# Score pairs read behind their products, one bank for transposed weights, and TensorE's rows as written, in the attention of an encoder layer

## The chip, the cores and the metric

The kernel runs on one core of a Trainium2 chip. The metric is the time of one execution on the device in microseconds (us), as the median of several runs; lower is better. A core has five engines that work side by side, each through its own queue of instructions in a fixed order: TensorE (PE in the profile, with its weight loads as PEld) multiplies matrices and transposes, VectorE (DVE), ScalarE (ACT) and GpSimd (POOL) work on elements, and SyncE (SP) issues transfers (DMAs). An instruction that needs another engine's result waits on a semaphore, and everything behind it in its queue waits with it. Products are written to PSUM, which the kernel cuts into eight banks of 128 x 512 numbers.

## The reference

One layer of an encoder for 1024 positions of 1024 features, in float32. A projection feeds two branches, a gated MLP (A) and eight heads of attention (B). Each head attends with three patterns of window and dilation, whose results are joined by their softmax denominators.

```python
PATTERNS = ((128, 1), (512, 4), (2048, 16))

def mixture_of_dilations(q, k, v):
    slopes = alibi_slopes(N_HEADS_B)
    outs, lses = [], []
    for _, dilation in PATTERNS:
        o, l = dilated_window_attention(q, k, v, dilation, slopes)
        outs.append(o)
        lses.append(l)
    w = jax.nn.softmax(jnp.stack(lses, axis=0), axis=0)
    o = jnp.stack(outs, axis=0)
    return jnp.sum(w[..., None].astype(o.dtype) * o, axis=0)

def hybrid_layer(x, w_in, b_gate, g_pre, g_post, ln_g, ln_b, w_s, b_s, w_pa, w_pb, w_o):
    h = rms_norm(x, g_pre)
    proj = h @ w_in
    u_a, v_a, z_a, q_b, k_b, v_b, z_b, gate_a, gate_b = jnp.split(proj, SPLIT_OFFS, axis=-1)
    y_a = spatial_gating(jax.nn.gelu(u_a), jax.nn.gelu(v_a), ln_g, ln_b, w_s, b_s) * jax.nn.silu(z_a)
    ...
    m = g_a * (y_a @ w_pa) + g_b * (y_b @ w_pb)
    return x + rms_norm(m @ w_o, g_post)
```

## The kernel before

Each float32 product is made of three products of halves: high times high, high times low, low times high. `split` (L158) makes the halves, the high one (names that end in h) on ACT at L159, the low one (l) on DVE or POOL at L160. The kernel first makes the projections, then runs the attention, and ends with the products by `w_pb` and `w_o` and the last norm. Beside the attention, whose rows on TensorE are short, it works off the product `y_a @ w_pa` of the MLP branch.

The eight banks of PSUM are handed out by name (L66): two to the MLP's sums (`mm`), three to scores (`sc`), one to transposes (`tp`) and two to the sums of weighted values (`pv`). A bank is free again when its last reader is done.

For each head h:

- `queries_keys` loads and splits q (`qr`, `qc`), and loads the halves of the keys (`krh`, `krl`, L595) and three tables of biases (`ta`, `te`, `tb`, L599).
- `scores` makes eight pairs of score tiles: six products (L662 to L664) for each pair, or twelve narrower ones for the last pair (first and last chunk). At L665 DVE adds the bias and takes the row's extreme; at L669 ACT takes the exponential and its sum, into the weights `st`. In the names, sc610 is the pair of head 6, first kind, tiles 0 and 1; the last pair reads the table `te`.
- `exchange` (L682) brings the extremes and sums of one pattern into the other's order with 16 small copies on POOL and 16 on DVE, `normalise` (L692 to L700) makes the joint factors `nm` on DVE, with an exponential `dd` on ACT, and `scale` (L706 to L710) multiplies the weights by them; eight tiles of it fall to DVE.
- `weigh` makes the weighted sum of values in nine stages. In each, `keys` (L724 to L732) transposes up to four tiles of weights with TensorE into one bank (L728), and splits it into `pth` (ACT) and `ptl` (DVE). Two stages later (`LAG`) the products with v follow, for the first four stages at L747 (sums `pr`), for the others at L762 (sums `pc`). The stages are called b0 to b3 (residues), a1 and a3 (chunks), e (ends), a5 and a7; with the head's number, pb30 is the first of head 3, pa25 the eighth of head 2.

`keys` takes its bank by turns from `tp` and from `sc`:

```python
                pt = bank(turn[0], f"p{name}")
                turn.reverse()
```

The loop at L900 to L926 writes the stages of head h with the score pairs of head h + 1 (`PAIRS`), the loads for head h + 2, and steps of the MLP (`BESIDE`) among them. A step is three products of 128 x 512 (L870 to L872) of a tile of w_pa with a quarter `ya` of the MLP's values; ya0310 is a quarter for the first half of the positions. The eighth, b = 1 in the names (ya1...), come later. Ahead of the loop, head 0's scores run among MLP steps alone.

The rows are not issued as written. A scheduler of the framework runs over the whole program with its own estimate of times, and sets the order of every engine's queue, TensorE's and SP's among them.

Of the kernel before, what the change touches and what calls it, by code (L numbers as in the profile page):

```python
# [13 lines left out]
ALU = mybir.AluOpType  # L14
# [9 lines left out]
H = 8  # L24
# [12 lines left out]
def tile_hybrid_encoder(  # L37
# [39 lines left out]
    def bank(tag, name):  # L77
        return psum.tile([P, 512], F32, tag=tag, bufs=BUFS[tag], name=name)
# [61 lines left out]
    def take(steps, n=None):  # L140

        while n is None or n > 0:
            if next(steps, steps) is steps:
                break
            if n is not None:
                n -= 1
# [433 lines left out]
    with tc.tile_pool(name="heads", bufs=1) as hp, tc.tile_pool(name="attn", bufs=1) as ap:  # L580
        def queries_keys(h, res):

            def pair(nm, shape):
                return [hp.tile([P] + shape, F32R, tag=f"{nm}{s}", name=f"{nm}{s}{h}") for s in "hl"]

            res["qr"], res["qc"], res["kr"] = pair("qr", [4, 256]), pair("qc", [8, P]), pair("kr", [4, 256])
            for b in range(2):
                t = wpool.tile([P, 512], F32, tag="ws", bufs=2, name=f"q{h}{b}")
                nc.sync.dma_start(t, q_d[h][:, 512 * b:512 * (b + 1)])
                split(*[w[:, :, b * P:(b + 1) * P] for w in res["qr"]], t.rearrange("p (j r) -> p r j", r=4))  # L590
                split(*[w[:, 4 * b:4 * b + 4, :].rearrange("p a (r i) -> p a r i", r=4) for w in res["qc"]],
                      t.rearrange("p (a i r) -> p a r i", a=4, r=4), nc.gpsimd)
                yield
            for s in range(2):
                nc.sync.dma_start(f32(res["kr"][s]), k_d[h][:, s])  # L595
                yield
            for x, terms, shape in (("ta", alibi_a, [P, 256]), ("te", alibi_e, [P, 2, 192]), ("tb", alibi_b, [P, 384])):
                res[x] = hp.tile(shape, F32, tag=x, name=f"{x}{h}")
                nc.sync.dma_start(res[x], terms[h])  # L599

        def residue_values(h, res):

            res["vb"] = []
            for s, vd in enumerate((v_hi, v_lo)):
                b_ = ap.tile([P, 4, 2, E], F32R, tag=f"vb{s}", name=f"vbt{s}{h}")
                vt_ = vd.rearrange("(b j r) n -> j r b n", b=2, r=4)
                for bb in range(2):
                    nc.sync.dma_start(f32(b_[:, :, bb, :]), vt_[:, :, bb, h * P:(h + 1) * P])
                res["vb"].append(b_)
# [16 lines left out]
        def scores(h, res):  # L626

            qr, qc, kr, ta, te, tb = [res[n] for n in ("qr", "qc", "kr", "ta", "te", "tb")]  # L630
            own = res["own"] = hp.tile([P, 2, 8, 2], F32, tag="own", bufs=2, name=f"own{h}")
            wts = res["wts"] = {}
            order = [(1, (i, i + 1)) for i in (0, 2, 4, 6)] + [(0, (1, 2)), (0, (3, 4)), (0, (5, 6)), (0, (0, 7))]
            for half, pair in order:
                ps = bank("sc", f"sc{h}{half}{pair[0]}").rearrange("p (t n) -> p t n", t=2)
                st = (hp if half else ap).tile([P, 2, 256], F32, tag=f"st{half}", bufs=7, name=f"st{h}{half}{pair[0]}")
                n = 256
                for t, idx in enumerate(pair):
                    if half:
                        b, r = divmod(idx, 4)  # L640
                        lhs = [w[:, r, b * P:(b + 1) * P] for w in qr]
                        blocks = [(0, 256, [w[:, r, :] for w in kr])]
                        bias = tb[:, P * (1 - b):P * (1 - b) + 256]
                    else:
                        lhs = [w[:, idx, :] for w in qc]
                        if idx in (0, 7):
                            w0, n, j0 = (64, 192, 0) if idx == 0 else (P, 192, 208)
                            blocks = [(0, w0, [w[:, :, j0:j0 + w0 // 4] for w in kr]),
                                      (w0, n - w0, [w[:, :, j0 + w0 // 4:j0 + n // 4] for w in kr])]
                            bias = te[:, t, :]  # L650
                        else:
                            j0 = 32 * idx - 16
                            blocks = [(0, 256, [w[:, :, j0:j0 + 64].rearrange("p r (u i) -> p u r i", u=2)
                                                for w in kr])]
                            bias = ta
                    for c0, w, rhs in blocks:
                        dst = ps[:, t, c0:c0 + w]
                        if len(rhs[0].shape) == 3:
                            dst = dst.rearrange("p (r i) -> p r i", r=4)
                        elif len(rhs[0].shape) == 4:  # L660
                            dst = dst.rearrange("p (u r i) -> p u r i", u=2, r=4)
                        nc.tensor.matmul(dst, lhs[0], rhs[0], start=True, stop=False)  # L662
                        nc.tensor.matmul(dst, lhs[0], rhs[1], start=False, stop=False)
                        nc.tensor.matmul(dst, lhs[1], rhs[0], start=False, stop=True)  # L664
                    nc.vector.tensor_tensor_reduce(st[:, t, :n], ps[:, t, :n], bias, -1.0, -NEG, ALU.add, ALU.min,  # L665
                                                   own[:, half, idx, 0:1])
                for t, idx in enumerate(pair):
                    wts[half, idx] = st[:, t, :n]
                    nc.scalar.activation(st[:, t, :n], st[:, t, :n], AF.Exp, bias=own[:, half, idx, 0:1], scale=-1.0,  # L669
                                         accum_out=own[:, half, idx, 1:2])  # L670
                yield
# [44 lines left out]
        def weigh(h, res):  # L716
# [5 lines left out]

            def keys(jobs, n, w, name):

                pt = bank(turn[0], f"p{name}")
                turn.reverse()
                for c0, src in jobs:
                    nc.tensor.transpose(pt[:n, c0:c0 + P], src, ident)  # L728
                hi = ap.tile([P, 512], F32R, tag="pth", bufs=LAG + 1, name=f"pth{name}")
                lo = ap.tile([P, 512], F32R, tag="ptl", bufs=LAG + 1, name=f"ptl{name}")  # L730
                split(hi[:n, :w], lo[:n, :w], pt[:n, :w])
                return hi, lo  # L732


            pr, turn = {}, ["tp", "sc"]

            def residue(r):
                pw = keys([(256 * kb + P * b, wts[1, 4 * b + r][:, kb * P:(kb + 1) * P])
# [143 lines left out]
        ya = {}  # L882
        take(mlp_tiles(0, 0, ya))
        steps = mlp_products(ya)
        heads = [{} for _ in range(H + 1)]
        take(queries_keys(0, heads[0]))
        take(steps, 8)
        residue_values(0, heads[0])
        chunk_values(0, heads[0])
        for _ in scores(0, heads[0]):  # L890
            take(steps, 1)
        take(exchange(0, heads[0], 0))
        take(exchange(0, heads[0], 1))
        normalise(0, heads[0])
        for tile_ in TILES[0] + TILES[1]:
            scale(heads[0], *tile_)
        for _ in queries_keys(1, heads[1]):
            take(steps, 3)
        before = iter(())
        for h in range(H):  # L900
            more = h + 1 < H
            pairs = scores(h + 1, heads[h + 1]) if more else iter(())
            ahead = queries_keys(h + 2, heads[h + 2]) if h + 2 < H else iter(())
            stages = weigh(h, heads[h])
            for i in range(9):
                take(stages, 1)
                take(before, 1)
                for j in range(BESIDE[i]):
                    if j < PAIRS[i]:
                        take(pairs, 1)  # L910
                    take(steps, 1)
                if i == 3 and more:
                    residue_values(h + 1, heads[h + 1])
                    take(exchange(h + 1, heads[h + 1], 0))
                    late = exchange(h + 1, heads[h + 1], 1)
                if more and i in (6, 7):
                    take(late, 1)
                if more and i == 8:
                    normalise(h + 1, heads[h + 1])
                    for tile_ in TILES[0] + TILES[1]:  # L920
                        scale(heads[h + 1], *tile_)
                    chunk_values(h + 1, heads[h + 1])
                if i > 4:
                    take(ahead, 1)
            take(ahead)
            before = stages  # L926
        for _ in before:
            take(steps, 3)


    with tc.tile_pool(name="tail", bufs=1) as tp:
# [147 lines left out]
```

## Time and profile before

| what | us |
| --- | --- |
| median of three runs | 1573.42 |
| lowest and highest run | 1571.92, 1582.71 |
| the profiled execution | 1580.57 |
| span of the profiled execution | 1578.8 |
| first transposes of weights of head 0 | start at 1058.65 |
| last transposes of weights of head 7 | start at 1364.3 |
| granted clock of TensorE, mean | 0.982 |

A row of the profile's timeline gives the start, the time until the end, the engine, the line, the operation, what it writes and reads, the shape, and in brackets how long the engine was idle ahead of it and what ended that. Names are without the numbers of heads there: all of pb00 to pb73 read "pb". A row of the waits names the waiting engine and line, what it waited for, and the total, the count and the longest. A window's row gives the busy time of each engine in that stretch, TensorE's granted clock, and the share of the DMA engines. Durations of products overlap: TensorE starts one product while the one before drains, so the step from start to start tells what a row costs.

### The profile page before, as it was taken

The numbers are of one execution on the slowest core, as the hardware profiler recorded it, in microseconds if no ns is written. First come the engines' busy times: TensorE is split into PE (matmuls) and PEld (weight loads), VectorE is DVE, ScalarE is ACT, GpSimd is POOL, SyncE is SP. The second block draws the span as 40 slices with busy tenths as digits, with TensorE's granted clock in tenths as the row PEclk, the third lists the DMA queues.
The fourth block names the chain that finished last, engine by engine and source line by source line (L and its number), as shares of the span: only waits on it lengthen the run. The fifth ranks groups of instructions, "written<-read, shape, count | busy, mean of one in ns | idle before, by whom it ended". The sixth has DMA issues, their size and how long they took to land.

```text
span 1578.8 us, 22737 instructions
## 1 busy us (share of the span) xinstructions
PE 1519.4 (96%) x7863; PEld 1280.5 (81%) x7863; DVE 862.8 (55%) x1698; ACT 688.2 (44%) x1315; POOL 778.6 (49%) x711
## 2 busy tenths in 40 slices
PE   8999999999999999999999999989998889999998
PEld 4787999988888888788788888867887778878886
DVE  5722544476665664856665555476667657232112
ACT  5522433343433434343444444576666656341111
POOL 2412644465655555555655555456444455473132
PEclk9999999999999999999999999999999989999999
DMA  8454333344534442535444343587676776885531
GB/s 260 156 172 173 128 107 102 111 127 130 170 117 150 133 162 94 168 121 160 139 132 129 125 148 113 163 245 234 196 205 173 201 226 180 227 278 166 194 107 67
DMA packets 247940, 252.16 MB, mean 160 GB/s; under 512 B 14312, under 2 KB 187400, under 8 KB 247568
## 3 DMA queue, kind: packets, MB, share of 16 engines
q1 hardware_dynamic: 247456, 249.88, 50.7%
q8 instruction: 62, 1.02, 0.3%
q10 hardware_dynamic: 368, 0.82, 0.2%
q14 instruction: 54, 0.44, 0.1%
HBM read 174.10 MB, written 76.55 MB: 159 GB/s over the span
## 4 chain that ended last, share of the span: by engine, by line
PE 72%; DVE 8%; issue 5%; ACT 4%; DMA 4%; POOL 3%; SPq 1%; DVEq 0%; ACTq 0%; POOLq 0%
PE pa L870 2%; PE pa L871 2%; PE pb L994 2%; PE pb L995 2%; PE pb L993 2%; PE pa L872 2%; PE sg L527 2%; PE vb L154 1%; PE vb L156 1%; PE vb L155 1%; ACT st L669 1%; POOL out L1014 1%; PE pr L747 1%; DMA vn<-v_d 1%; DVE vn L516 1%
## 5 line engine op out<-in xcount | busy, mean ns | idle before, releaser
L108 POOL TENSOR_TENSOR wl_pa<-wr_pa,wh_pa 128x512 fp32r<-128x512 f32 x56 | 72.6, 1308 | 61.7 <-ACT wh_pa L106 53.3
L669 ACT ACTIVATE st<-st,own 128x256 f32<-128x256 f32 (+1 forms) x128 | 63.0, 493 | 38.4 <-DVE own L665 37.9
L516 DVE TENSOR_SCALAR vn<-vn,mean,rstd 128x128 f32<-128x128 f32 x128 | 54.9, 483 | 36.9 <-DMA vn<-v_d 36.5
L993 PE MATMUL pb<-yh,wh_pb 128*128 128x512 f32 x128 | 50.0, 390 | 1.7 <-ACT yh L159 1.7
L994 PE MATMUL pb<-yl,wh_pb 128*128 128x512 f32 x128 | 50.1, 391 | 0.4 <-DVE yl L160 0.2
L106 ACT ACTIVATE wh_pa<-wr_pa 128x512 fp32r<-128x512 f32 x64 | 38.6, 625 | 26.6 <-PE pa L871 12.6
L995 PE MATMUL pb<-yh,wl_pb 128*128 128x512 f32 x128 | 49.8, 389 | 0.0
L1028 ACT ACTIVATE sq<-o 128x512 f32<-128x512 f32 x16 | 9.6, 598 | 74.7 <-PE o L1026 74.7
L160 POOL TENSOR_TENSOR vl<-vn,vh 128x512 fp32r<-128x512 f32 x32 | 41.3, 1291 | 0.8 <-ACT vh L159 0.8
L665 DVE CUSTOM_DVE_ANT_0 st<-sc,tb 128x256 f32<-128x256 f32 x64 | 25.5, 421 | 28.9 <-PE sc L664 23.6
L997 POOL TENSOR_TENSOR mb<-thb,mb 128x512 f32<-128x512 f32 x16 | 20.6, 1287 | 41.8 <-DVE thb L996 32.2
L682 DVE COPY oth<-own 32x4 f32<-32x4 f32 x128 | 34.3, 268 | 12.3 <-ACT st L669 10.6
L160 POOL TENSOR_TENSOR qcl<-q,qch 128x512 fp32r<-128x512 f32 x16 | 27.9, 1756 | 26.3 <-ACT qch L159 26.3
L728 PE MATMUL pb<-ident,st 128*128 128x128 f32 x128 | 23.3, 294 | 16.2 <-DVE ptla L160 11.5
L815 POOL TENSOR_TENSOR o<-o,zt 128x512 f32<-128x512 f32 x16 | 20.6, 1295 | 36.2 <-DMA zt<-z_d 18.0
L1008 DVE TENSOR_TENSOR sso<-sso 128x1 f32<-128x1 f32 x8 | 1.3, 160 | 67.6 <-ACT sq L1028 67.6
L682 POOL COPY oth<-own 32x4 f32<-32x4 f32 x128 | 23.9, 187 | 24.3 <-ACT st L669 19.4
L728 PEld LDWEIGHTS pb<-ident,st 128*128 128x128 f32 x128 | 16.7, 150 | 21.9 <-DVE ptla L160 13.2
L165 POOL TENSOR_TENSOR sso<-sso,mhalf 128x1 f32<-128x1 f32 x8 | 4.4, 550 | 59.1 <-DVE sso L164 59.1
L108 POOL TENSOR_TENSOR wl_wos<-wr_wos,wh_wos 128x512 fp32r<-128x512 f32 x16 | 20.7, 1292 | 22.8 <-ACT wh_wos L106 22.8
L160 DVE TENSOR_TENSOR ptlb<-pb,pthb 128x512 fp32r<-128x512 f32 x32 | 21.9, 688 | 16.3 <-ACT pthb L159 16.1
L108 POOL TENSOR_TENSOR wl_vb<-wr_vb,wh_vb 128x512 fp32r<-128x512 f32 x14 | 18.2, 1310 | 25.0 <-ACT wh_vb L106 25.0
(2643 smaller groups left out, 5870.6 us busy)
## 6 DMA issues: line engine op xcount, KB each, us to landing
wr_pa<-in_w_proj_a_dram SPq DMA_DIRECT2D x32, 512.0 KB, 5.1
wr_g<-in_w_in_dram SPq DMA_DIRECT2D x16, 512.0 KB, 3.7
wr_va<-in_w_in_dram SPq DMA_DIRECT2D x16, 512.0 KB, 3.7
wr_u<-in_w_in_dram SPq DMA_DIRECT2D x16, 512.0 KB, 4.1
wr_z<-in_w_in_dram SPq DMA_DIRECT2D x16, 512.0 KB, 3.8
vn<-v_d SPq DMA_DIRECT2D x32, 256.0 KB, 2.7
y_d<-s SPq DMA_DIRECT2D x32, 256.0 KB, 3.1
wr_yf<-y_d SPq DMA_DIRECT2D x16, 512.0 KB, 6.3
```

The costliest lines, as they stand in the source:

```text
L106: nc.scalar.activation(hi, src, AF.Copy)
L108: low.tensor_tensor(lo, src, f32(hi), ALU.subtract)
L160: low.tensor_tensor(lo, src, f32(hi), ALU.subtract)
L516: nc.vector.tensor_scalar(vn[:, c, :], vn[:, c, :], mean[:, 4 * b + c, 0:1], rstd[:, 4 * b + c:4 * b + c + 1], op0=ALU.subtract, op1=ALU.mult)
L527: nc.tensor.matmul(pg[:, 256 * c:256 * (c + 1)], w[:, 2 * cp + c, :], wst, start=(w is vh and c == 0), stop=(w is vl and c == 1), skip_gro ...
L669: nc.scalar.activation(st[:, t, :n], st[:, t, :n], AF.Exp, bias=own[:, half, idx, 0:1], scale=-1.0, accum_out=own[:, half, idx, 1:2])
L682: (nc.gpsimd, nc.vector)[half].tensor_copy(dst, src)
L728: nc.tensor.transpose(pt[:n, c0:c0 + P], src, ident)
L870: nc.tensor.matmul(pss[m], lh[:, k, :], rh, start=(q == 0 and k == 0), stop=False)
L993: nc.tensor.matmul(ps, lh, rh, start=(k == 0), stop=False)
L994: nc.tensor.matmul(ps, lh, rl, start=False, stop=False)
L995: nc.tensor.matmul(ps, ll, rh, start=False, stop=(k == KT - 1))
```

## The change

Three things change, all in the attention.

1. `scores` multiplies both tiles of a pair before DVE reads either. Before, the read of the first tile stood between the two tiles' products.
2. `keys` always takes the bank `tp`. The three banks `sc` then serve scores alone, and each stage's transposes have to wait until the subtraction `ptl` of the stage before has read the bank.
3. From the loads of head 0 to the last stage of head 7, TensorE's queue has the order in which the program is written. The scheduler still orders the other engines' queues. The loop is moved into the block without a change.

```diff
@@ scores
-                n = 256
+                n, biases = 256, []
                 for t, idx in enumerate(pair):
...
                         nc.tensor.matmul(dst, lhs[1], rhs[0], start=False, stop=True)
-                    nc.vector.tensor_tensor_reduce(st[:, t, :n], ps[:, t, :n], bias, -1.0, -NEG, ALU.add, ALU.min,
+                    biases.append(bias)
+                for t, idx in enumerate(pair):
+                    nc.vector.tensor_tensor_reduce(st[:, t, :n], ps[:, t, :n], biases[t], -1.0, -NEG, ALU.add, ALU.min,
                                                    own[:, half, idx, 0:1])
@@ keys
-                pt = bank(turn[0], f"p{name}")
-                turn.reverse()
+                pt = bank("tp", f"p{name}")
...
-            pr, turn = {}, ["tp", "sc"]
+            pr = {}
@@ the loop over the heads
-        heads = [{} for _ in range(H + 1)]
-        take(queries_keys(0, heads[0]))
...
+        with tc.manual_schedule(engines={mybir.EngineType.PE}):
+            heads = [{} for _ in range(H + 1)]
+            take(queries_keys(0, heads[0]))
...
```

Lines behind the two added ones in `scores` move by one or two numbers: L728 becomes L729, L870 to L872 become L871 to L873.

What this does to the queues shows at three places. The first is TensorE's queue ahead of head 0's first transposes (pb00), before; the names in it are the MLP's sums (pa00, pa01), the quarters ya0201 and ya0310, and the weights wh and wl.

```order
L872 MATMUL pa01_9839<-ya0201h_9758,wl_pa0110_9749 128x512
L728 MATMUL pb00_10109<-ident_69,st010_9828 128x128 [waits DVE_49]
L747 MATMUL pr00_10201<-pthb00_10114,vbt10_9803 128x256 [waits DMAHW3_49]
L728 MATMUL pb02_10192<-ident_69,st012_9844 128x128 [waits DVE_49]
L747 MATMUL pr00_10201<-ptlb00_10115,vbt00_9800 128x256 x2
L870 MATMUL pa00_9751<-ya0310h_9858,wh_pa0011_9741 128x512 [waits Activation_49]
L871 MATMUL pa00_9751<-ya0310l_9859,wh_pa0011_9741 128x512 [waits DVE_49]
L872 MATMUL pa00_9751<-ya0310h_9858,wl_pa0011_9743 128x512
```

The same place in the change:

```order
L871 MATMUL pa00_9753<-ya0310h_9860,wh_pa0011_9743 128x512 [waits Activation_49]
L872 MATMUL pa00_9753<-ya0310l_9861,wh_pa0011_9743 128x512 [waits Pool_49]
L873 MATMUL pa00_9753<-ya0310h_9860,wl_pa0011_9745 128x512
L871 MATMUL pa01_9841<-ya0201h_9760,wh_pa0110_9749 128x512
L873 MATMUL pa01_9841<-ya0201h_9760,wl_pa0110_9751 128x512
L729 MATMUL pb00_10111<-ident_69,st010_9830 128x128
L662 MATMUL sc110_10123<-krh1_10032,qrh1_10028 128x256 [waits DMAHW2_49,PE_49]
L663 MATMUL sc110_10123<-krl1_10033,qrh1_10028 128x256 [waits DMAHW4_49]
```

The 12 products with ya0310 moved from behind pb00 and pb02 to ahead of the 12 of pa01 with ya0201, so 36 MLP products stand between head 0's last scores and pb00 where 24 stood; the scores of head 1 follow pb00 directly.

The second place is TensorE's queue at the end of head 2, from the stage a5 to the first stage of head 3, before:

```order
L728 MATMUL pa25_11394<-ident_69,st203_10732 128x128
L762 MATMUL pc20_11359<-ptla23_11299,va02_11006 128x256
L872 MATMUL pa06_11426<-ya0000h_9661,wl_pa0600_10950 128x512
L728 MATMUL pa27_11439<-ident_69,st205_10751 128x128 [waits DVE_49]
L762 MATMUL pc21_11360<-ptle2_11356,ve02_11007 128x128
L728 MATMUL pb30_11508<-ident_69,st310_11057 128x128 [waits DVE_49]
```

and in the change:

```order
L729 MATMUL pa25_11396<-ident_69,st203_10734 128x128 [waits DVE_49]
L763 MATMUL pc20_11361<-ptla23_11301,va02_11008 128x256
L873 MATMUL pa06_11428<-ya0000h_9661,wl_pa0600_10952 128x512
L729 MATMUL pa27_11441<-ident_69,st205_10753 128x128 [waits DVE_49]
L763 MATMUL pc21_11362<-ptle2_11358,ve02_11009 128x128
L729 MATMUL pb30_11510<-ident_69,st310_11059 128x128 [waits DVE_49]
```

The rows stand as before, but the waits are for other work. pa25 now waits for ptle2, pa27 for ptla25 (before for ptle2), and pb30 for ptla27 (before for ptla25).

The third place is SP's queue of transfers for heads 5 and 6, before:

```order
L595 DMA krh6_12336<-k_d_90 128x1024 [waits DMAHW0_49,PE_49]
L622 DMA ve05_12480<-vb_h_84 16x2x128 [waits PE_49]
L621 DMA va05_12479<-vb_h_84 32x7x128 [waits DMAHW3_49,PE_49]
L621 DMA va15_12489<-vb_l_85 32x7x128 [waits DMAHW7_49]
L622 DMA ve15_12490<-vb_l_85 16x2x128 [waits DMAHW0_49]
L595 DMA krl6_12337<-k_d_90 128x1024 [waits DMAHW1_49]
```

and in the change:

```order
L595 DMA krh6_12338<-k_d_90 128x1024 [waits DMAHW0_49,PE_49]
L622 DMA ve05_12482<-vb_h_84 16x2x128 [waits PE_49]
L622 DMA ve15_12492<-vb_l_85 16x2x128 [waits DMAHW0_49]
L595 DMA krl6_12339<-k_d_90 128x1024 [waits DMAHW1_49]
L599 DMA te6_12504<-in_alibi_e_dram 128x384 [waits DMAHW3_49]
L621 DMA va05_12481<-vb_h_84 32x7x128 [waits DMAHW3_49,PE_49]
```

The eight loads va moved from ahead of krl6 to behind it; the eight loads ve stay ahead of it, and the first of them waits for the products pc of head 4 that end before pb50. On TensorE the pair sc610, which needs krh6 and krl6, stood behind pb50, the products pc41 and 13 MLP products, with its rows that need krl6 further back; it moved to directly behind pb50 and six of the products pc41.

More of the change, by code (lines that the diff above doesn't have):

```diff
@@ L884, in tile_hybrid_encoder @@
         steps = mlp_products(ya)
-        heads = [{} for _ in range(H + 1)]
-        take(queries_keys(0, heads[0]))
[L887 to L926, printed above, removed]
@@ L927, in tile_hybrid_encoder @@
-        for _ in before:
-            take(steps, 3)
+        with tc.manual_schedule(engines={mybir.EngineType.PE}):
+            heads = [{} for _ in range(H + 1)]
+            take(queries_keys(0, heads[0]))
+            take(steps, 8)
+            residue_values(0, heads[0])
+            chunk_values(0, heads[0])
+            for _ in scores(0, heads[0]):
+                take(steps, 1)
+            take(exchange(0, heads[0], 0))
+            take(exchange(0, heads[0], 1))
+            normalise(0, heads[0])
+            for tile_ in TILES[0] + TILES[1]:
+                scale(heads[0], *tile_)
+            for _ in queries_keys(1, heads[1]):
+                take(steps, 3)
+            before = iter(())
+            for h in range(H):
+                more = h + 1 < H
+                pairs = scores(h + 1, heads[h + 1]) if more else iter(())
+                ahead = queries_keys(h + 2, heads[h + 2]) if h + 2 < H else iter(())
+                stages = weigh(h, heads[h])
+                for i in range(9):
+                    take(stages, 1)
+                    take(before, 1)
+                    for j in range(BESIDE[i]):
+                        if j < PAIRS[i]:
+                            take(pairs, 1)
+                        take(steps, 1)
+                    if i == 3 and more:
+                        residue_values(h + 1, heads[h + 1])
+                        take(exchange(h + 1, heads[h + 1], 0))
+                        late = exchange(h + 1, heads[h + 1], 1)
+                    if more and i in (6, 7):
+                        take(late, 1)
+                    if more and i == 8:
+                        normalise(h + 1, heads[h + 1])
+                        for tile_ in TILES[0] + TILES[1]:
+                            scale(heads[h + 1], *tile_)
+                        chunk_values(h + 1, heads[h + 1])
+                    if i > 4:
+                        take(ahead, 1)
+                take(ahead)
+                before = stages
+            for _ in before:
+                take(steps, 3)
```

## Prediction

> **What bounds the kernel now.** I read the page first: busy time by engine, then the chain that ended last.
>
> ```profile
> span 1578.8 us, 22737 instructions
> PE 1519.4 (96%) x7863; PEld 1280.5 (81%) x7863; DVE 862.8 (55%) x1698; ACT 688.2 (44%) x1315; POOL 778.6 (49%) x711
> PE 72%; DVE 8%; issue 5%; ACT 4%; DMA 4%; POOL 3%; SPq 1%; DVEq 0%; ACTq 0%; POOLq 0%
> ```
>
> TensorE (PE) is busy for 96% of the span and no other engine for more than 55%: the kernel is bound by TensorE's rows, and only gaps between them can be won or lost. The change touches the attention alone, 1028 to 1365 us, so the next view is busy time and granted clock there, by 40 us.
>
> ```profile
> 1100.00:1140.00 40.00, 38.62 (x238) 32.55 (x237) 26.96 (x84) 26.62 (x65) 19.92 (x30) 1.00 0.63 191
> 1180.00:1220.00 40.00, 33.20 (x200) 28.27 (x200) 29.66 (x79) 26.77 (x63) 20.12 (x29) 0.93 0.65 185
> sum 360.00, PE 328.48 PEld 277.18 DVE 231.69 ACT 226.06 POOL 182.73; mean PE 36.50 PEld 30.80 DVE 25.74 ACT 25.12 POOL 20.30
> ```
>
> The columns are the stretch, its length, the busy time of PE, weight loads, DVE, ACT and POOL, then PE's clock. TensorE idles 360 - 328.48 = 31.5 us in these nine stretches, which is all that a better order could take out directly. What it waits for, from 880 to 1340 us:
>
> ```profile
> PE pb L728 <- DVE ptla L160: 11.5, 4, 6.6
> PE sc L662 <- DVE own L665: 7.4, 7, 3.3
> PE pb L728 <- DVE st L708: 4.6, 2, 4.2
> PE pa L871 <- DVE ya1310l L160: 2.1, 2, 1.8
> ```
>
> (total, times, longest). The first and third stand at a head's start, where its first transposes wait for VectorE (DVE). The second is the read between the two tiles of a score pair, which the change moves. Waits have a second price, seen in windows laid around them:
>
> ```profile
> 1056.60:1064.20 7.60, 4.85 (x17) 3.88 (x18) 6.49 (x18) 6.01 (x14) 3.70 (x5) 0.55 0.79 269
> 1137.00:1146.00 9.00, 7.81 (x49) 6.45 (x48) 5.15 (x16) 5.57 (x16) 3.81 (x3) 1.00 0.60 170
> 1174.80:1180.30 5.50, 4.67 (x23) 4.38 (x24) 2.89 (x9) 1.92 (x6) 3.81 (x3) 0.69 0.47 132
> 1213.00:1221.30 8.30, 3.23 (x14) 3.17 (x15) 6.31 (x9) 2.67 (x6) 4.01 (x4) 0.59 0.22 65
> ```
>
> ```profile
> 1103.52 0.38 PE L728 MATMUL pb<-ident,st 128*128 128x128 f32 x2
> 1139.17 0.33 PE L728 MATMUL pb<-ident,st 128*128 128x128 f32 x1 [0.93 <-DVE ptla L160]
> ```
>
> Around the waits of 4.24, 2.00 (rows in the terms below) and 6.6 us, at 1058.65, 1175.63 and 1218 us, the granted clock is 0.55, 0.69 and 0.59; around the 0.93 us at 1139.17 it stays 1.00. Length times (1 - clock) gives the lost clock: 3.4, 1.7 and 3.4 us.
>
> **Term 1: the start of the attention.** In written order TensorE comes to the 12 products with ya0310 before the 12 of pa01 with ya0201 and before the first transposes pb00. Before, it skipped them. These rows give the times:
>
> ```profile
> 1054.02 0.39 PE L872 MATMUL pa<-ya0201h,wl_pa 128*128 128x512 f32 x1
> 1058.65 1.39 PE L728 MATMUL pb<-ident,st 128*128 128x128 f32 x4 [4.24 <-DVE st L708]
> 1060.57 0.90 ACT L710 ACTIVATE st<-st,nm 128x256 f32<-128x256 f32 x2
> 1061.37 2.17 ACT L159 ACTIVATE ya0310h<-wr_yf 128x512 fp32r<-128x512 f32 x4
> 1062.58 2.98 POOL L160 TENSOR_TENSOR ya0310l<-wr_yf,ya0310h 128x512 fp32r<-128x512 f32 x2 [2.43 <-ACT ya0310h L159]
> 1064.33 0.57 SPq L595 DMA_DIRECT2D krl<-k_d  x1
> 1070.06 0.27 PE L663 MATMUL sc<-krl,qrh 128*128 128x256 f32 x1
> DMA to landing us min/median/max: 5.6/7.4/7.5
> ```
>
> The last ya0201 product starts at 1054.02; 12 products at 0.23 us apart (as at 1169.69 and 1169.92 in the rows of head 2 below) take 2.75 us, so TensorE now arrives at ya0310 at about 1051.5. ScalarE (ACT) makes ya0310h at 1061.37; the change moves pthb00 from ahead of it, which gives it 0.6 us: 1060.8. POOL's second low half ends 1062.58 + 2.98 - 0.6 = 1065.0. So 9.3 us of idling take the place of 4.24, and the last ya0310 product ends at 1065.3. Behind it stand 2.75 us of pa01 and then pb00, at 1068.1 instead of 1058.65. The score pair sc110 follows, whose krl1 was issued at 1064.33 behind a load of weights that waits for POOL's first ya0310l; 0.6 us earlier plus the landing of 5.6 to 7.5 us (last row, for krh, the same kind and size) is 1069.3 to 1071.2, middle 1070.3. Before, the same product ran at 1070.06, but with 13 MLP products, 8 transposes, 6 products with vb and one of scores more behind it: 13 x 0.23 + 8 x 0.09 (a quarter of the step from one four of transposes to the next product) + 7 x 0.12 (half width, half the step) = 4.5 us of work. **+4.7 us.** Ends: 0, if the head absorbs it (it took 1103.52 - 1058.65 = 44.9 us, and a head's rows at these steps, 72 MLP products, 48 of scores, 34 transposes and 50 products with v, are 31.6 us), and +8, with 3.4 us of clock lost as around the 4.24 us wait.
>
> **Term 2: score pairs.** Nothing is added: the same reads, only behind both tiles' six products. The first read starts three products (3 x 0.12 = 0.36 us) later, the second earlier by the first's wait.
>
> ```profile
> 1231.81 0.69 DVE L160 TENSOR_TENSOR ya1111l<-wr_yf,ya1111h 128x512 fp32r<-128x512 f32 x1 [3.93 <-ACT ya1111h L159]
> ```
>
> The 7.4 us of waits go, except the longest, 3.3 us, which ends at the read behind this split: DVE itself was held for 3.93 us there, and the next pair's bank would wait instead. **-4.1 us**; ends -7.4 and 0.
>
> **Term 3: one bank for the transposes of weights.** Every stage's transposes now wait for VectorE's subtraction ptl of the stage before. Where the stages are 3.6 us apart that is done in time: 0.60 us of transposes, ScalarE's copy and 0.68 us of ptl (rows below) make some 2 us. At a head's end it is not, because VectorE runs the exchange, the normalising and eight scales of the next head between ptl of "ends" (ptle) and ptla5. Head 2:
>
> ```profile
> 1168.44 0.41 DVE L160 TENSOR_TENSOR ptle<-pe,pthe 64x256 fp32r<-64x256 f32 x1
> 1171.21 2.58 DVE L708 TENSOR_SCALAR st<-st,nm 128x256 f32<-128x256 f32 x7
> 1173.71 0.68 DVE L160 TENSOR_TENSOR ptla<-pa,ptha 128x512 fp32r<-128x512 f32 x1
> 1166.61 0.60 PE L728 MATMUL pa<-ident,st 128*128 128x128 f32 x4
> 1169.69 0.39 PE L871 MATMUL pa<-ya0000l,wh_pa 128*128 128x512 f32 x1
> 1169.92 0.40 PE L872 MATMUL pa<-ya0000h,wl_pa 128*128 128x512 f32 x1
> 1170.15 0.38 PE L728 MATMUL pa<-ident,st 128*128 128x128 f32 x2
> 1173.23 0.40 PE L872 MATMUL pa<-ya0000h,wl_pa 128*128 128x512 f32 x1
> 1175.63 0.66 PE L728 MATMUL pb<-ident,st 128*128 128x128 f32 x4 [2.00 <-DVE ptla L160]
> ```
>
> The transposes pa5 began at 1166.61 and would now wait for ptle's end at 1168.85: 2.2 us. Those of pa7 began at 1170.15 and would wait for ptla5's end at 1174.39. From them to the end of the last product ahead of pb pass 1173.23 + 0.23 - 1170.15 = 3.3 us (two transposes, six small products, nine of the MLP), so the next head's pb starts at 1177.7 rather than 1175.63: +2.1. The wait at pb, 2.00 us, is gone, since its ptl follows pa7 sooner than that. So one wait is not removed but moved ahead of 3.3 us of work. The same reading gives +0.5, +2.2, +1.7 and +0.8 for heads 0, 1, 3 and 4, together 7.3. One scale of some 0.35 us (seven take 2.58) moves from behind ptla5 to ahead of it, 1.7 us over five heads. **+9.0 us.** Half-clocked stretches I hold equal, one long wait a head as before. Ends: 0, if the pairs of term 2 bring the last scores earlier by that much, and 5 x 3.3 = +16.5.
>
> A rule to weigh here: the Trainium skill, "TensorE: Matmul & The Clock Gate", Part 1, says that the array goes to half clock after an idle window of about 3.4 us. This trace differs: 2.00 us of waiting were enough for 0.69 at 1175, so the measured row decides. By the page, waits of 2 us such as those that term 3 makes would cost no clock at all; the sum above holds without it, and the slow rival (b) is where it matters.
>
> **Term 4: the scores of head 6, in order.** Their keys krh6 and krl6 come late:
>
> ```profile
> 1261.47 0.38 SPq L595 DMA_DIRECT2D krh<-k_d  x1
> 1261.90 0.99 SPq L622 DMA_DIRECT2D ve<-vb_h  x2
> 1273.37 0.42 SPq L595 DMA_DIRECT2D krl<-k_d  x1
> 1283.06 0.28 PE L663 MATMUL sc<-krl,qrh 128*128 128x256 f32 x1
> 1259.05 0.33 PE L728 MATMUL pb<-ident,st 128*128 128x128 f32 x1 [2.04 <-DVE ptla L160]
> 1340.86 0.27 PE L728 MATMUL pb<-ident,st 128*128 128x128 f32 x1
> ```
>
> Before, the scheduler's order had TensorE do MLP products until 1283, and the scores followed. In written order sc610 stands 1.1 us behind pb50. By terms 1 to 3 pb50 moves from 1259.05 to 1268.7. In the queue of SyncE (SP), krl6 now stands ahead of the eight va loads, behind eight ve loads of 0.48 us each, which start when TensorE is nine MLP products, 2.1 us, short of pb50: 1266.6 + 3.8 = 1270.4, and with 5.6 to 7.5 us it lands at about 1277.0. TensorE, there at 1269.8, stalls 7.2 us, and loses 3.4 us of clock. From pb50 to pb70 before: 1340.86 - 1259.05 = 81.8 us, for 63.3 us of rows. After: 1.1 + 7.2 + 3.4 + 62.1, and 7.5 us of the ordinary losses of two heads (heads 1 and 2, from 1103.52 to 1139.17 and to 1175.63 us, took 4 and 5 us over their 31.6): 81.3. **-0.5 us**, ends -7 (krl6 there in time) and +5 (the stall not offset by fewer waits later).
>
> **The sum:** 4.7 - 4.1 + 9.0 - 0.5 = +9.1 us. The profiled execution took 1580.57 us (span 1578.8), 7 above the median of 1573.42. The change would make it 1589.7, and against the median **1582 us**, +0.6%.
>
> **The rivals.**
> (b) Slower: the stalls add up. pa5 and pa7 are two waits where pb was one, each over 2 us with 1.7 us of clock as at 1175, which is 8.5 us more for the second waits of five heads. For: head 3, whose end cost 6.6 us already. Against: during the first wait's slow stretch the second is partly paid. With terms 1 and 3 at their upper ends (8 + 16.5), 8.5 us of clock, -4.1 and -0.5 it is +28: 1602 us. It decides once ptla5 ends over 4 us behind TensorE's arrival at pa7 in most heads.
> By that rule of the Trainium skill the 8.5 us would not be there, and it would come to an estimated 1593 us.
>
> (c) Faster: VectorE's queue at the head's end comes forward, because the te pair is multiplied without the wait between its tiles and the exchange starts earlier. Then the waits at pb (11.5 + 4.6) and at scores (7.4) go, with 8.5 us of clock around them: -32; with term 1 kept -27; between half of that and all, -20: 1553 us. Against: the copies, nm and scales from 1167 to 1174 us depend on ScalarE's exponentials too, which the change leaves.
> (d) The change does little: rows of heads 1 to 3 stand on TensorE almost as before, and a late bank costs what pb cost. Then 1573 us.
>
> **How the numbers follow.** The forecast, 1582, has 0.42; (b) 0.27; (c) 0.19; (d) 0.12. One per cent of 1573 is 15.7 us, about what a measurement of this kernel tells from no change: faster is below 1557.7, slower above 1589.2. (c) gives 0.14 to faster and 0.05 to same; (d) is same; of the forecast 0.37 are same and 0.05, its terms at their upper ends, slower, as all of (b) is. Same 0.54, slower 0.32, faster 0.14. The range, 1555 to 1603, leaves out the lower half of (c) and the upper part of (b).
>
> **What would show it.** Term 1: a PE wait near 1052 to 1061 us at L871 or L872 for ya0310. Term 2: no row "sc <- DVE own" of more than a few tenths. Term 3: waits of 1 to 5 us at L729 pa <- DVE ptle and ptla, none at pb. Term 4: a wait of sc for a DMA of krl, some 7 us, in the period of head 5. It would be wrong if pb stays a wait, or if ya0310 or krl6 arrive before TensorE does.

## The result, and the profile after

| | before | changed |
| --- | --- | --- |
| median | 1572.72 us | 1591.91 us |
| lowest and highest run | 1571.92, 1582.71 | 1590.52, 1593.87 |
| profiled execution, its span | 1580.57, 1578.8 us | 1591.04, 1589.3 us |

The changed kernel is slower: the ratio of the times is 1.0102, 95% interval 1.0083 to 1.0121. Its forecast was 1582 us, its range 1555 to 1603. From the one profiled execution to the other it is +10.5 us, from median to median +19: the execution profiled before was one of the slower ones of its kernel.

The page after, its span, its busy line and its chain:

```profile
span 1589.3 us, 22762 instructions
PE 1513.0 (95%) x7863; PEld 1277.7 (80%) x7863; DVE 856.3 (54%) x1698; ACT 689.9 (43%) x1315; POOL 778.5 (49%) x711
PE 73%; DVE 8%; issue 5%; DMA 4%; ACT 4%; POOL 3%; SPq 0%; ACTq 0%; DVEq 0%; POOLq 0%
```

TensorE does the same number of rows and is busy for no longer; what grew is its idle time. The main waits of TensorE after, from 880 to 1380 us (total, times, longest):

```profile
PE pa L729 <- DVE ptle L160: 15.0, 6, 3.4
PE pa L729 <- DVE ptla L160: 10.2, 6, 3.3
PE pa L871 <- ACT ya0310h L159: 10.1, 1, 10.1
PE pb L729 <- DVE ptla L160: 4.9, 1, 4.9
PE sc L663 <- DMA krl<-k_d: 4.0, 1, 4.0
PE pb L729 <- DVE ptlb L160: 2.0, 2, 1.2
PE sc L662 <- DVE own L667: 0.7, 2, 0.4
```

The waits of pb for VectorE fell from 16.1 us (ptla and st) to 6.9 (ptla and ptlb), those of sc for the reads from 7.4 to 0.7. In their place stand 25.2 us at pa for the bank, 10.1 us for ya0310 and 4.0 us for krl. The end of head 2 on the timeline after, VectorE first and then TensorE:

```profile
1167.96 2.70 DVE L684 COPY oth<-own 32x4 f32<-32x4 f32 x8 [0.84 <-ACT st L671]
1171.15 0.41 DVE L160 TENSOR_TENSOR ptle<-pe,pthe 64x256 fp32r<-64x256 f32 x1
1172.53 3.89 DVE L710 TENSOR_SCALAR st<-st,nm 128x256 f32<-128x256 f32 x8
1176.34 0.68 DVE L160 TENSOR_TENSOR ptla<-pa,ptha 128x512 fp32r<-128x512 f32 x1
1171.61 0.66 PE L729 MATMUL pa<-ident,st 128*128 128x128 f32 x4 [2.52 <-DVE ptle L160]
1177.08 0.44 PE L729 MATMUL pa<-ident,st 128*128 128x128 f32 x2 [1.72 <-DVE ptla L160]
1180.47 0.60 PE L729 MATMUL pb<-ident,st 128*128 128x128 f32 x4
```

pa5 starts 0.05 us after ptle's end at 1171.56, and pa7 0.06 us after ptla5's at 1177.02. VectorE's queue is what TensorE follows here. From pa7 to pb pass 3.4 us, in which nothing waits.

### The profile page after: what moved, and what is told of

The parts are those of the page before. It is cut to its first block, busy times and chain, and to the rows that moved or that the text cites. A ratio compares the mean times of both kernels' runs of the same rounds, so it can differ in the third digit from the quotient of the medians.

```text
span 1589.3 us, 22762 instructions
## 1 busy us (share of the span) xinstructions
PE 1513.0 (95%) x7863; PEld 1277.7 (80%) x7863; DVE 856.3 (54%) x1698; ACT 689.9 (43%) x1315; POOL 778.5 (49%) x711
## 4 chain that ended last, share of the span: by engine, by line
PE 73%; DVE 8%; issue 5%; DMA 4%; ACT 4%; POOL 3%; SPq 0%; ACTq 0%; DVEq 0%; POOLq 0%
PE pa L871 2%; PE pa L872 2%; PE pb L996 2%; PE pb L997 2%; PE pb L995 2%; PE pa L873 2%; PE sg L527 2%; PE vb L154 1%; PE vb L156 1%; PE vb L155 1%; DVE oth L684 1%; PE pc L763 1%; PE pr L748 1%; POOL out L1016 1%; DVE st L710 1%
## 5 line engine op out<-in xcount | busy, mean ns | idle before, releaser
L516 DVE TENSOR_SCALAR vn<-vn,mean,rstd 128x128 f32<-128x128 f32 x128 | 57.7, 505 | 36.6 <-DMA vn<-v_d 36.3
L106 ACT ACTIVATE wh_pa<-wr_pa 128x512 fp32r<-128x512 f32 x64 | 39.2, 626 | 43.1 <-PE pa L872 34.6
L997 PE MATMUL pb<-yh,wl_pb 128*128 128x512 f32 x128 | 50.5, 394 | 0.0
L729 PE MATMUL pa<-ident,st 128*128 128x128 f32 x112 | 18.5, 282 | 25.2 <-DVE ptle L160 15.0
L729 PEld LDWEIGHTS pa<-ident,st 128*128 128x128 f32 x112 | 13.2, 142 | 33.5 <-DVE ptle L160 17.6
L160 DVE TENSOR_TENSOR ptla<-pa,ptha 128x512 fp32r<-128x512 f32 (+1 forms) x32 | 19.9, 621 | 21.4 <-ACT ptha L159 21.3
L710 DVE TENSOR_SCALAR st<-st,nm 128x256 f32<-128x256 f32 x64 | 31.2, 555 | 0.3
```

The lines of the kernel that those rows point to most:

```text
L106: nc.scalar.activation(hi, src, AF.Copy)
L160: low.tensor_tensor(lo, src, f32(hi), ALU.subtract)
L516: nc.vector.tensor_scalar(vn[:, c, :], vn[:, c, :], mean[:, 4 * b + c, 0:1], rstd[:, 4 * b + c:4 * b + c + 1], op0=ALU.subtract, op1=ALU.mult)
L710: nc.vector.tensor_scalar(w, w, f, None, op0=ALU.mult)
L997: nc.tensor.matmul(ps, ll, rh, start=False, stop=(k == KT - 1))
```

## The experiments

The three edits can be made apart. The first four kernels undo or do them one by one; every ratio is against the kernel before on the same chip. The kernels ran on more than one chip, so where two of them are compared the ratios decide.

**Pairs alone.** The edit is the diff's first part, on the kernel before.

```diff
+                    biases.append(bias)
+                for t, idx in enumerate(pair):
+                    nc.vector.tensor_tensor_reduce(st[:, t, :n], ps[:, t, :n], biases[t], -1.0, -NEG, ALU.add, ALU.min,
```

> Pairs multiplied ahead of their reads alone; two banks in turns and the scheduler's order stay. Theory A (the cost of the change is the single bank, about +9 us, and the pairs give 4 us back): about 4 us faster than before, 1566 to 1571 us, and the wait 'sc <- DVE own' falls from 7.4 to under 4 us. Rival B (the cost is the written order, which stops TensorE ahead of late data): the same here, -4 us. Rival C (reading a pair late holds the score banks longer and delays the exchange): slower by 3 us or more.

Measured: 1569.9 us, ratio 0.9971 (0.9960 to 0.9982), 4.6 us faster. Theory A and rival B forecast the same here, and rival C falls. Its waits, two rows:

```profile
PE pb L730 <- DVE ptla L160: 15.6, 5, 7.5
PE sc L662 <- DVE own L667: 0.8, 2, 0.4
```

The read's wait is down from 7.4 to 0.8 us; the wait at pb for ptla does not go (11.5 us before).

**One bank alone.**

```diff
-                pt = bank(turn[0], f"p{name}")
-                turn.reverse()
+                pt = bank("tp", f"p{name}")
...
```

> One bank for the transposes of weights alone; reads between the tiles and the scheduler's order stay. Theory A: 8 to 15 us slower than before, with waits of pa for ptle and ptla of 15 us or more together. Rival B: within 4 us of before, since the scheduler moves other rows ahead of the waiting transposes.

Measured: 1598.12 us, ratio 1.0154 (1.0138 to 1.0170), +24 us, more than theory A's upper end. Its waits, two rows:

```profile
PE pa L727 <- DVE ptle L160: 9.7, 4, 2.9
PE pa L727 <- DVE ptla L160: 8.7, 7, 3.3
```

They are 18.4 us together, as theory A said. Rival B falls.

**Written order alone.**

```diff
+        with tc.manual_schedule(engines={mybir.EngineType.PE}):
...
```

> TensorE's rows as written alone; two banks in turns and the reads between the tiles stay. Theory A: 0 to 5 us slower than before (ya0310 is waited for some 10 us, but the first head takes most of it back). Rival B: 10 to 15 us slower, with waits for ya0310 of 10 us and for krl of 4 us or more that are not taken back.

Measured: 1616.3 us, ratio 1.0278 (1.0252 to 1.0304), +44 us. Both theories missed it. Its longest waits:

```profile
PE sc L662 <- DVE own L665: 57.7, 64, 3.0
PE pa L870 <- ACT ya0310h L159: 2.6, 1, 2.6
```

All 64 pairs wait, 0.9 us each, for VectorE's read between their two tiles. Before, the scheduler put other rows there and 7.4 us were left. Rival B's place, ya0310 and krl, is not where the time goes.

**Pairs and written order, two banks.** The changed kernel with `turn` restored.

> The changed kernel with two banks in turns again: pairs and written order, without the single bank. Theory A: 9 us or more faster than the changed kernel, about level with before (1570 to 1578 us); the waits of pa for ptle and ptla are gone. Rival B: still 10 us slower than before.

Measured: 1574.01 us, ratio 0.9997 (0.9986 to 1.0009). As theory A said: level with before, 16.5 us under the changed kernel by the ratios, and rival B falls. Against pairs alone it is 0.26% slower, some 4 us, and the two intervals do not touch: the written order is not free. Its waits:

```profile
PE pb L730 <- DVE ptla L160: 15.5, 5, 7.5
PE pa L872 <- ACT ya0310h L159: 10.0, 1, 10.0
PE sc L662 <- DMA krh<-k_d: 6.5, 1, 6.5
PE sc L663 <- DMA krl<-k_d: 4.0, 1, 4.0
```

The wait for ya0310 is as long as in the changed kernel, 10 us, and yet the kernel is level. No row of pa for ptle or ptla is left.

**Pairs and one bank, the scheduler's order.**

> Pairs and the single bank, with the scheduler's order on TensorE. Theory A (the single bank costs some 16 to 23 us whatever sets the order): 1585 to 1595 us, 1.0 to 1.5% slower than before, with the steady heads 1 and 2 some 3 us longer than with pairs alone (34.7 and 35.4 us). Rival D (the bank costs only where the order is fixed, since the scheduler can put other rows ahead): within 5 us of pairs alone, 1567 to 1575 us.

Measured: 1600.44 us, ratio 1.0168 (1.0154 to 1.0183), 30 us above pairs alone. Rival D falls: the scheduler's order is no cover for a missing bank. Theory A has the sign and the steady heads right, and too low a price. TensorE waits 13.6 us at pa for ptle and 7.4 for ptla. Heads 1 and 2 take 37.9 and 38.9 us, 3.1 and 3.5 more than with pairs alone. But by the start of head 7 (pb70) the kernel is 26.7 us behind pairs alone, and most of that lies in heads 0 and 6, 9.5 and 14.9 us longer. With one bank alone, too, head 6 takes 42.9 us instead of 32.0. With pairs and one bank, TensorE's waits in head 6 are 7.3 us, and why it takes so much longer stays open.

**The changed kernel, with one stage of nine on a score bank.**

```diff
-                pt = bank("tp", f"p{name}")
+                pt = bank("sc" if name[0] == "a" and name[-1] == "5" else "tp", f"p{name}")
```

> The changed kernel with one stage in nine, a5, on a score bank; the other eight stay on the single bank. Theory A (the bank costs at a head's end alone, where pa5 waits for ptle and pa7 for ptla5): nearly all of the loss comes back, 1573 to 1579 us, and the waits of pa for ptle and ptla fall from 25 us to under 6; the waits of pb for ptla return, some 15 us. Rival E (each of the nine stages loses a little to the single bank): at most a third comes back, 1585 to 1590 us.

Measured: 1579.89 us, ratio 1.0044 (1.0032 to 1.0056). From 1.0102 down to the 0.9997 of pairs with written order there are 1.05%, 16.5 us; 0.58% of it, 9 us (6 to 13 by the intervals), came back: less than theory A said, more than rival E allows. The waits:

```profile
PE pb L729 <- DVE ptla L160: 22.1, 5, 9.0
PE pa L729 <- DVE ptla L160: 1.1, 1, 1.1
```

The table shows where. It gives the start of each head's first transposes (pb) on the timelines, and from it the length of each head's period, in us:

| kernel | pb00 | head 0 | 1 | 2 | 3 | 4 | 5 | 6 | pb70 |
| --- | --- | --- | --- | --- | --- | --- | --- | --- | --- |
| before | 1058.7 | 44.9 | 35.7 | 36.5 | 42.4 | 41.0 | 49.8 | 32.0 | 1340.9 |
| changed | 1064.9 | 39.5 | 38.2 | 37.8 | 44.7 | 43.2 | 45.8 | 33.6 | 1347.8 |
| pairs alone | 1056.3 | 42.1 | 34.7 | 35.4 | 42.4 | 38.4 | 49.8 | 30.7 | 1329.9 |
| pairs, written | 1066.8 | 32.3 | 34.7 | 35.4 | 42.4 | 38.4 | 48.2 | 34.7 | 1332.9 |
| changed, a5 on sc | 1068.9 | 34.6 | 34.7 | 35.4 | 41.2 | 46.0 | 42.6 | 33.2 | 1336.5 |

Heads 1 to 3 are back to the periods with two banks or better, by one stage in nine: in them the whole price of the single bank is paid at the head's end. What did not come back lies in the start (2.1 us), head 0 (2.3) and head 4 (7.6), of which heads 3, 5 and 6 win back 8.3 by pb70. At the end of head 4 pb waits 9.0 us for ptla, where with pairs and written order it waits 2.4. The timelines show why. VectorE's queue, which the scheduler orders, has five rows between the scales and that last split of the head, ptla47: ya1310l and qrl, twice each, and one sum o; ScalarE's has their high halves ahead of ptha47. So ptla47 starts 9.2 us behind ptla45 (1250.91 and 1260.13 us). With pairs and written order these rows stand behind ptla47, and it starts 2.7 us behind ptla45. In the changed kernel they stand ahead of it as well (1258.54 and 1267.80 us).

**The changed kernel, written order from the loop on.** Head 0's scores and the steps around them are left to the scheduler.

> The changed kernel with the written order on TensorE only from the loop over the heads on; head 0's scores and the MLP products around them are left to the scheduler. The wait of 10 us for ya0310 goes. Theory A (the first head takes back most of what is lost there): 0 to 3 us faster than the changed kernel, 1588 to 1592 us. Rival F (those 10 us are lost for good): 7 to 10 us faster, 1581 to 1585 us.

Measured: 1590.68 us, ratio 1.0110 (1.0097 to 1.0123). Theory A holds: it is the changed kernel's 1.0102 within the scatter of both. pb00 comes at 1056.0 instead of 1064.9, but head 0 takes 50.5 us instead of 39.5, so the first transposes of head 1 come 2 us later.

**Pairs and written order, keys first.** In `queries_keys` the loads of the two halves of the keys are written ahead of those of q.

```diff
+            for s in range(2):
+                nc.sync.dma_start(f32(res["kr"][s]), k_d[h][:, s])
+                yield
             for b in range(2):
...
-            for s in range(2):
-                nc.sync.dma_start(f32(res["kr"][s]), k_d[h][:, s])
-                yield
```

> Pairs and written order with two banks, and the loads of the keys written ahead of those of the queries, so that krh6 and krl6 stand five places earlier in SP's queue. Theory A (the waits of sc for krh6 and krl6, 6.5 and 4.0 us, are real losses): 5 to 10 us faster than pairs and written order (1574.0), 1564 to 1569 us. Rival G (the period of head 5 is bound by the transfers and splits behind them anyway): within 3 us of 1574, with the waits found at another load.

Measured: 1570.62 us, ratio 0.9974 (0.9963 to 0.9986), 3.4 us under the kernel without it: between rival G's 3 us and theory A's 5, and with the intervals of both kernels (1 to 6 us) it decides for neither. The waits for keys are gone, and one for the queries' split has come, as rival G said:

```profile
PE pa L872 <- ACT ya0310h L159: 9.9, 1, 9.9
PE sc L662 <- ACT qrh L159: 9.1, 2, 7.1
```

**Written order and one bank, reads between the tiles.** The eighth corner.

> Written order and the single bank, with the reads between the tiles: the eighth corner of the three edits. Theory A (the bank adds some 16 us to any order, and TensorE pays for each read between two tiles once its rows are fixed): 1616 + 10 to 20, so 1626 to 1640 us, with waits of sc for own of 45 to 60 us. Rival H (the waits at the reads give VectorE the time to free the bank, so the two costs overlap): within 6 us of written order alone, 1610 to 1622 us.

Measured: 1637.99 us, ratio 1.0389 (1.0363 to 1.0416), 22 us above written order alone by the medians (1.1% by the ratios), in theory A's range. The reads cost what they cost without the single bank:

```profile
PE sc L662 <- DVE own L665: 57.9, 64, 3.0
PE pa L727 <- DVE ptle L160: 8.5, 6, 2.0
```

So the three edits in all their combinations, as ratios to before:

| | scheduler's order | written order |
| --- | --- | --- |
| two banks, read between | 1 | 1.0278 |
| two banks, pairs | 0.9971 | 0.9997 |
| one bank, read between | 1.0154 | 1.0389 |
| one bank, pairs | 1.0168 | 1.0102 |

The single bank costs in every column, 1.0 to 2.0% of the time. Where the scheduler sets the order, the pairs gain 0.3% with two banks and nothing with one; where it is fixed, they gain 2.8 to 2.9%. The written order costs 2.3 to 2.8% with the read between the tiles and 0.3% with pairs and two banks; with pairs and one bank it gains 0.7%.

**Better than both.** Three kernels leave out the single bank. The first has pairs, the scheduler's order, and keys first.

> Pairs, two banks, the scheduler's order, and the keys' loads written ahead of the queries'. Theory A (late keys of head 6 cost the period of head 5 some 10 us in the scheduler's order as well, 49.8 us where other periods take 35 to 42): 5 to 9 us faster than pairs alone, 1561 to 1565 us. Rival G (the keys come earlier, but the queries later by as much): within 3 us of 1570.

Measured: 1566.47 us, ratio 0.9942 (0.9927 to 0.9958), 3.4 us under pairs alone (4.6 by the ratios, 2 to 8 by their intervals): between the theories again, and again deciding for neither. Head 5 went from 49.8 to 45.5 us.

The second also keeps the banks' turns from head to head. Nine stages are an odd number, so a7 and the next head's b0 shared the bank `tp` before.

```diff
+        turn = ["tp", "sc"]
+
         def weigh(h, res):
...
-            pr, turn = {}, ["tp", "sc"]
+            pr = {}
```

> The same, and the turns of the two banks go on from head to head, so that the first transposes of every other head no longer wait for the last split of the head before. Theory A (pb waits for the bank, 15.6 us with pairs alone): another 3 to 8 us faster than pairs and keys first. Rival I (pb waits for its own scaled weights almost as long): within 2 us.

Measured: 1556.75 us, ratio 0.9882 (0.9867 to 0.9898): 9.7 us better still, more than theory A said. Its longest waits of the attention:

```profile
PE pb L732 <- DVE st L710: 5.1, 1, 5.1
PE sc L662 <- DVE own L667: 2.6, 2, 2.4
PE pa L732 <- DVE own L667: 2.2, 1, 2.2
```

The wait of pb for ptla, 12.8 us in the kernel without it, is not among them. This is the fastest kernel run, 1.2% faster than before.

The third adds the written order from the loop on.

> The same as the one before, with the written order on TensorE from the loop over the heads on. Theory A (with two banks and pairs the written order is neither gain nor loss): within 4 us of the kernel before it. Rival B: 5 us or more slower.

Measured: 1567.88 us, ratio 0.9949 (0.9934 to 0.9964), 11 us slower than the second. Here rival B is right, and the longest wait shows where TensorE stands:

```profile
PE sc L662 <- ACT qrh L159: 13.0, 3, 9.6
PE pb L732 <- DVE st L710: 5.1, 1, 5.1
```

With the keys' loads ahead, the queries' come later, and in written order TensorE stands in front of their split, 13.0 us in all. In the scheduler's order no such row is among the longest. Theory A took the written order for neither gain nor loss with pairs and two banks; it had cost 0.26% there already.

## Why the prediction was right, and where it was short

The time lies in the range, and the sign of the sum was right. Against the profiled execution it was close: +9.1 us forecast, +10.5 measured. That closeness is luck: the execution profiled before was 8 us above its median, which hides what the sum lacks. Against the medians the sum had half: +9 forecast, +16 by the ratio. Which of that execution's waits a median run does not have, no profile here shows.

By the ratios, one edit after the other, the pairs give 4.6 us, the written order behind them costs 4.1, and the single bank on top of both 16.5. The sum had 4.1, 4.2 (terms 1 and 4 together) and 9.0, so the third term is the one that was short. That terms 1 and 4 come out together is luck as well. In the traces of pairs alone and of pairs with written order, the start and head 0 cost 0.6 us by pb10, head 5 gives 1.6 back, head 6 costs 4.0, and 3.3 us come behind pb70, where no term looks (238.1 us from pb70 to the end of the span, and 241.4). Why these two places cost that was not tried.

**Term 2, the pairs** (-4.1 us): right. Alone they gave 4.6 us.

**Term 1, the start** (+4.7 us): the wait was read rightly and its price was not. The timeline after:

```profile
1057.45 0.79 PE L871 MATMUL pa<-ya0310h,wh_pa 128*128 128x512 f32 x1 [10.09 <-ACT ya0310h L159]
1056.79 2.18 ACT L159 ACTIVATE ya0310h<-wr_yf 128x512 fp32r<-128x512 f32 x4
1064.94 0.60 PE L729 MATMUL pb<-ident,st 128*128 128x128 f32 x4
1065.49 0.29 PE L663 MATMUL sc<-krl,qrh 128*128 128x256 f32 x1
```

The wait is 10.09 us where I had 9.3. But ya0310h was made at 1056.8 and not at 1060.8: TensorE and ScalarE both came there some 4 us earlier. So pb00 stood at 1064.9 rather than 1068.1, and the keys krl1 had landed. The head took the rest back: with written order and pairs pb00 comes 10.5 us later than with pairs alone, and the next head's pb 0.6 us later. The value was near the lower end of the term, 0.

**Term 3, the single bank** (+9.0 us): the mechanism was right in place and sign for heads 1 to 3, and the term is the one mis-sized. It measured 1.0102 - 0.9997, 1.05% or 16.5 us, its upper end. For head 2 I forecast waits of 2.2 us at pa5 and then one at pa7; they are 2.52 and 1.72. Against pairs and written order, heads 1 to 3 lost 3.5, 2.4 and 2.3 us, 8.2 together, where I had 7.0 with the moved scales. The miss is in heads 0 and 4: 7.2 and 4.8 us, where I had 0.9 and 1.2. (The start and heads 5 and 6 took 5.3 us back, so 14.9 are left by pb70.)

In head 0 the step that failed is that the stages stand 3.6 us apart and find the bank free. With pairs and written order two pairs of its stages stand 2.5 us apart, and there the changed kernel waits 1.19 us for ptlb and 1.46 for ptla; at the head's end it waits 1.10 and 1.70. The trace of before could not show this price, since its head 0 took 44.9 us for other reasons: the single bank alone leaves pb10 where it was (1102.9 us, before 1103.5), while on top of pairs alone it moves it from 1098.5 to 1107.1.

In head 4 the step that failed is that VectorE's queue keeps its order there. The scheduler put four splits and a sum ahead of ptla47, as told above, and the wait at pb50 was 4.9 us, where I had none: one of my signs of being wrong, that pb stays a wait, did show at this place.

**Term 4, head 6's keys** (-0.5 us): right within 2 us. The rows after:

```profile
1268.35 0.45 PE L729 MATMUL pb<-ident,st 128*128 128x128 f32 x1 [4.88 <-DVE ptla L160]
1270.40 0.42 SPq L595 DMA_DIRECT2D krl<-k_d  x1
1274.91 0.58 PE L663 MATMUL sc<-krl,qrh 128*128 128x256 f32 x1 [3.99 <-DMA krl<-k_d]
1347.81 0.27 PE L729 MATMUL pb<-ident,st 128*128 128x128 f32 x1
```

pb50 at 1268.35 (forecast 1268.7), krl6 issued at 1270.40 (forecast 1270.4), landed within 4.5 us rather than 6.6, so TensorE stalled 4.0 us and not 7.2. From pb50 to pb70 it took 79.5 us; I had 81.3.

**The rivals.** (b) did not come, since the waits at pa5 and pa7 were not followed by half clock in every head: in heads 1 and 2 the granted clock stayed 1.00. Those at pa7 were at most 3.3 us, under its 4. (c) fell: with pairs alone the waits at pb stay, 15.6 us for ptla and 4.8 for st, and in the changed kernel most of them moved to pa. (d) fell for the change as a whole; its number is that of pairs with written order and two banks (0.9997), where no bank is missing. What no part of the prediction saw is how the edits lean on each other: written order costs 2.3 to 2.8% without the pairs.

## What to carry to other kernels

A bank fewer is priced at the places where its reader is late, here mostly a head's end behind VectorE's queue, and in the written order one stage in nine on another bank won about half of it back. Before you fix an engine's order, look for rows in it that wait for another engine's step: here the scheduler had hidden all but 7.4 us of 57.7. With two banks the written order never gained, even without those rows (0.3% slower with pairs, 0.7% with pairs, keys first and the turns kept). And when several edits come together, price each against the kernel that the others leave, not against the trace of before: what hides a wait there may be what another edit takes away.

## What the runs showed of the hardware that was not expected

The length of a wait alone does not tell whether half clock follows. In the windows after, around the ends of heads 2 and 3 (the columns as in the prediction's windows; the clock stands ahead of the last two numbers):

```profile
1169.60:1180.50 10.90, 7.17 (x40) 5.75 (x41) 8.68 (x28) 4.65 (x12) 5.89 (x5) 1.00 0.87 274
1207.00:1225.00 18.00, 11.43 (x40) 9.02 (x40) 13.98 (x31) 7.57 (x15) 9.29 (x8) 0.72 0.50 170
```

Waits of 2.52 and 1.72 us left the clock at 1.00 in head 2, while one of 2.00 us was followed by 0.69 before; with waits of 3.3 us twice in head 3 it was 0.72. Before, the slow stretch did not start with the wait's end at 1175.63 us but over 1 us behind it, and lasted some 3 us: products of 128x512 stand 0.42 us apart at 1177.45 and 1177.87, and 0.23 again from 1180.38. The Trainium skill, "TensorE: Matmul & The Clock Gate", Part 1, says that activity is judged in a window of some 3.4 us that runs freely. A wait that falls across two windows would then be shared between them. That fits head 2's rows, but it leaves open why 2.00 us, less than one window, were enough before, and no run here was made to test it.
